# A two-layer hybrid decoder trunk on one core: x also passed transposed, packed weights, and the up-projection's products in another order

## The chip, the core and the metric

The kernel runs on one core of a Trainium2 chip. The metric is the device time of one execution in microseconds (us). A core has a matrix engine (TensorE, PE in the profile, with its weight loads as a row of their own, PEld), a vector engine (DVE), a scalar engine (ACT), GpSimd (POOL) and SyncE (SP), which here issues most of the DMA transfers. All of them run their own instruction lists in order and wait for each other through semaphores.

## What is computed

Two layers over 256 tokens of width 2048. Cut to what the change touches:

```python
def mixer_sublayer(x, ...):
    h = rms_norm(x, attn_norm)
    proj = h @ w_in                       # 12 blocks of columns: q, k, v of three groups of heads,
    (a_q, a_k, a_v, a_f, b_q, b_k, b_v,   # and the latents of the fourth:
     c_q, c_k, c_v, d_cq, d_ckv, d_kr) = jnp.split(proj, offsets, axis=-1)
    ...
    o_d = mla_attention(d_cq, d_ckv, d_kr, ...)   # q = rms_norm(c_q) @ w_uq, kv = rms_norm(c_kv) @ w_ukv
    ...
    return x + y @ w_out

def ffn_sublayer(x, ffn_norm, w_up, conv_w, conv_b, w_down):
    h = rms_norm(x, ffn_norm)
    u = causal_depthwise_conv(h @ w_up, conv_w, conv_b)      # 2048 -> 2 x 5632
    gate, val = jnp.split(u, 2, axis=-1)
    return x + (jax.nn.silu(gate) * val) @ w_down
```

Everything is float32.

## The kernel before

Each float32 factor of a large product is split into a high part and a rest, both in the type fp32r: high = copy of the value in fp32r, low = value minus high. A product of two such factors is then three products on TensorE: high by high, low by high, high by low. Of the weights, ACT makes the high part (line 226) and DVE the low part (line 227), two k-tiles of 128 rows at a time; of the activations, ACT and DVE do the same for hTs (lines 189 and 190), which holds h transposed: for each of 16 k-tiles 128 partitions by [high 256 tokens | low 256 tokens].

**The general product** is the class Gemm (lines 230 to 256). Tokens stand on the output's partitions, two tiles of 128, and up to 512 columns of weights stream through. For each k-tile and each token tile it issues lines 248, 249 and 250.

**The up-projection** is the function up (lines 802 to 825). It has the roles swapped: 128 columns of weights are loaded into the array and the tokens stream through. For each k-tile and each of four column blocks c there is a wide product, the high weights against [high | low] of hTs, 512 columns, and a narrow one, the low weights against high alone, 256 columns, both summed into the bank acc[c]. The two stand in turn, wide, narrow, for c = 0 to 3 (line 812); at the last k-tile the narrow one comes first. There are 22 calls of up in a layer (11 for the gate, tiles up_g, and 11 for the values, up_v), and each issues 16 x 8 = 128 products.

**The start of layer 0** (lines 466 to 485): the block lat (the latents of keys and values, the rotary key and the forget gate, 324 columns) comes first, then dq (the query latent, 512 columns), then aq, uq, ukv, ak and the rest. x is loaded in four chunks of 512 columns in its own layout (line 469), transposed by TensorE (line 201, 32 products), and split by ACT and DVE. For each chunk ACT also sums the squares (line 292) for the norm's factor r_in; that factor is applied when a product leaves its bank. In layer 1 the order of the products is the same, and h comes from the layer before.

**What sets the order.** The code is written as generators (tasks) from which each Gemm and each up takes one or two steps per pair of k-tiles, so that small work (transposes, norms, attention) lies between the large products. A scheduler then orders each engine's instructions. Transfers of weights are issued by SP, one per four k-tiles (line 260), into three buffers raw; the first weights lat0 come in pieces of two k-tiles (lines 222 and 223), each in two transfers, since the four columns of the forget gate lie elsewhere in w_in (lines 461 and 463). A row of a weight tile is a run of 2 KB in memory (512 columns), of 1280 and 16 bytes for lat.

Before the first data are there, TensorE runs 16 products on a tile of zeros, warm (line 105).

Of the kernel before, what the change touches and what calls it, by code (L numbers as in the profile page):

```python
# [24 lines left out]
L = 2  # L25
# [12 lines left out]
OFF_AQ, OFF_AK, OFF_AV, OFF_AF = 0, 512, 1024, 1536  # L38
OFF_BQ, OFF_BK, OFF_BV = 1540, 2052, 2564
OFF_CQ, OFF_CK, OFF_CV = 3076, 3588, 4100  # L40
OFF_DQ, OFF_DKV = 4612, 5124
# [33 lines left out]
def tile_trunk(ctx: ExitStack, tc: tile.TileContext, x, pvec, rows, ctab,  # L75
               w_in, w_uq, w_ukv, w_out, w_up, w_down, out):
# [13 lines left out]
    nc.sync.dma_start(pv[:, 0:KT], pvec[:, 0:KT])  # L90
# [13 lines left out]
    for _ in range(16):  # L104
        nc.tensor.matmul(wps[:, 0:256], warm[:, 0:P], warm, start=True, stop=True)
# [82 lines left out]
    def split_T(ps, j, gain, hi, lo):  # L188
        nc.scalar.activation(hi, ps[:, j * SEQ:(j + 1) * SEQ], AF.Identity, scale=gain)
        nc.vector.scalar_tensor_tensor(lo, ps[:, j * SEQ:(j + 1) * SEQ], gain, hi.bitcast(F32),  # L190
                                       op0=ALU.mult, op1=ALU.subtract)

    def transpose_split(src, n, cnt, gain, kt0, dh, dl):

        for j0 in range(0, cnt, 2):
# [7 lines left out]
            for j in (j0, j0 + 1):  # L203
                split_T(ps, j - j0, gain(j), dh[:, kt0 + j, :], dl[:, kt0 + j, :])
# [6 lines left out]
    def load_weights(src, k, n, nk):  # L211
        loaded[n, k] = wraw.tile([P, 4, 512], F32, tag="raw", name=f"raw_{n}_{k}")
        if n != "lat0":
            src(loaded[n, k], k, min(4, nk))

    def split_weights(src, k, N, n, nk):
# [9 lines left out]
        nc.scalar.copy(hi[:, :, :N], raw[:, :, :N])  # L226
        nc.vector.tensor_tensor(lo[:, :, :N], raw[:, :, :N], hi[:, :, :N].bitcast(F32), op=ALU.subtract)  # L227
        return hi, lo

    class Gemm:  # L230
# [7 lines left out]
        def steps(self, k0, cnt):  # L238
            N = self.N
            for g0 in range(k0, k0 + cnt, 2):  # L240
                hi, lo = split_weights(self.wsrc, g0, N, self.n, self.nk)
                parts = [(*self.act(g0 + i), hi[:, i, :N], lo[:, i, :N]) for i in range(2)]
                for t in range(NT):
                    o = self.acc[t][:, :N]
                    for i, (ah, al, wh, wl_) in enumerate(parts):
                        first, last = self.done + i == 0, self.done + i == self.nk - 1
                        sh, sl = ah[:, t * P:(t + 1) * P], al[:, t * P:(t + 1) * P]
                        nc.tensor.matmul(o, sh, wh, start=first, stop=False)  # L248
                        nc.tensor.matmul(o, sl, wh, start=False, stop=False)  # L249
                        last_mm[0] = nc.tensor.matmul(o, sh, wl_, start=False, stop=last)  # L250
# [43 lines left out]
    def x_ready(c, n, gname, l, ssq, r, rb=None):  # L294
# [3 lines left out]
        yield  # L298
        for t in range(NT):
# [155 lines left out]
    for l in range(L):  # L455
        wl = w_in[l]


        def lat_src(raw, k, cnt):
            rows_ = wl[k * P:(k + cnt) * P]  # L460
            nc.sync.dma_start(raw[:, :, :LATW],
                              rows_[:, OFF_DKV:OFF_DKV + LATW].rearrange("(a p) n -> p a n", p=P))
            nc.sync.dma_start(raw[:, :, LATW:LATF],
                              rows_[:, OFF_AF:OFF_AF + H].rearrange("(a p) n -> p a n", p=P))
        lat_gemm = Gemm(f"lat{l}", LATF, hT, lat_src, KT)
        for c in range(4):
            if l == 0:
# [7 lines left out]
        if l == 0:  # L475
            load_weights(wcols(wl, OFF_DQ, QR), 0, "dq0", KT)
            nc.sync.dma_start(pv[:, KT:], pvec[:, KT:])
            load_rows(0)
# [463 lines left out]
```

## Time and profile before

| | us |
|---|---|
| median of 3 runs | 2268.99 (2268.87 to 2269.32) |
| the profiled execution, its own time | 2267.43 |
| its span (first to last instruction) | 2265.3 |
| TensorE busy in it | 2257.2 |
| ScalarE / VectorE busy | 1197.3 / 1515.4 |

Rows of the timeline give an instruction's start and how long it took from there. On TensorE the products overlap: one that streams 512 columns is listed with 0.39 us while the next starts 0.23 us later. So the pace of TensorE is read from the difference between two starts, not from the listed durations. "x8" in a row means eight products in a row that read alike. The windows view sums busy time over a stretch; its count of products includes those that overlap its edges.

### The profile page before, as it was taken

The page shows a single profiled execution, that of the slowest core. Times are in us where ns is not written, and L with a number is a line of the kernel's source. Part 1 is how long each engine was busy: PE and PEld are TensorE (multiplying, and loading weights), DVE is VectorE, ACT ScalarE, POOL GpSimd, SP SyncE. Part 2 cuts the span into 40 slices and gives each one's busy share as a digit, 9 for nine tenths or more (in the row PEclk, how much of TensorE's full clock was granted, in tenths as well). Part 3 has the DMA queues.
Part 4 walks back from the last instruction along what each step waited for, and adds up shares of the span by engine and source line. Part 5 has one row for each costly group of instructions (what it writes and reads, how often), then busy time and mean ns, then how long its engine had stood idle before and what let it go on. Part 6 is the DMA issues. An engine that isn't in the chain of part 4 may idle for free.

```text
span 2265.3 us, 29605 instructions
## 1 busy us (share of the span) xinstructions
PE 2257.2 (100%) x11632; PEld 1913.5 (84%) x11632; DVE 1515.4 (67%) x2206; ACT 1197.3 (53%) x1738; POOL 1.2 (0%) x7
## 2 busy tenths in 40 slices
PE   9999999999999999999999999999999999999999
PEld 7888888888888888888888888888888888888887
DVE  5766875677656766577657658667776476755674
ACT  6555545555435554455555555455554355534552
POOL 0000000000000000000000000000000000000000
PEclk9999999999999999999999999999999999999999
DMA  7545445555565555555565445455555555555554
GB/s 261 185 143 165 161 159 186 181 191 183 189 195 192 181 192 188 186 190 182 176 191 191 137 161 168 154 183 178 191 187 197 193 185 187 186 191 190 195 168 167
DMA packets 213467, 412.72 MB, mean 182 GB/s; under 512 B 11088, under 2 KB 16464, under 8 KB 213328
## 3 DMA queue, kind: packets, MB, share of 16 engines
q1 hardware_dynamic: 212752, 409.79, 55.0%
q8 instruction: 91, 1.49, 0.3%
q10 hardware_dynamic: 576, 1.05, 0.1%
q14 instruction: 48, 0.39, 0.0%
HBM read 408.71 MB, written 2.10 MB: 181 GB/s over the span
## 4 chain that ended last, share of the span: by engine, by line
PE 99%; DVE 0%; ACT 0%; SPq 0%; DMA 0%; issue 0%; ACTq 0%; DVEq 0%
PE up_v L819 22%; PE up_g L819 22%; PE acc_dn L248 7%; PE acc_dn L250 7%; PE acc_dn L249 7%; PE acc_out L250 2%; PE acc_out L248 2%; PE acc_out L249 2%; PE acc_bk L250 1%; PE acc_cq L250 1%; PE acc_bk L248 1%; PE acc_av L248 1%; PE acc_av L250 1%; PE acc_cq L248 1%; PE acc_bq L248 1%; PE acc_cq L249 1%
## 5 line engine op out<-in xcount | busy, mean ns | idle before, releaser
L819 PE MATMUL up_g<-hTs,hi_g 128*128 128x512 f32 x1408 | 498.4, 398 | 0.0
L819 PE MATMUL up_v<-hTs,hi_v 128*128 128x512 f32 x1408 | 498.1, 398 | 0.0
L819 PE MATMUL up_v<-hTs,lo_v 128*128 128x256 f32 x1408 | 391.7, 281 | 0.0
L819 PE MATMUL up_g<-hTs,lo_g 128*128 128x256 f32 x1408 | 391.2, 280 | 0.0
L227 DVE TENSOR_TENSOR lo_dn<-raw_dn,hi_dn 128x1024 fp32r<-128x1024 f32 x176 | 214.5, 1224 | 190.4 <-ACT hi_dn L226 190.4
L819 PEld LDWEIGHTS up_v<-hTs,hi_v 128*128 128x128 f32 x1408 | 264.5, 188 | 62.9
L819 PEld LDWEIGHTS up_g<-hTs,hi_g 128*128 128x128 f32 x1408 | 264.5, 188 | 62.9
L227 DVE TENSOR_TENSOR lo_v<-raw_v,hi_v 128x1024 fp32r<-128x1024 f32 x176 | 213.4, 1223 | 155.2 <-ACT hi_v L226 155.2
L226 ACT CAST hi_dn<-raw_dn 128x1024 fp32r<-128x1024 f32 x176 | 185.3, 1053 | 243.6 <-PE acc_dn L249 211.2
L227 DVE TENSOR_TENSOR lo_g<-raw_g,hi_g 128x1024 fp32r<-128x1024 f32 x176 | 213.9, 1223 | 136.5 <-ACT hi_g L226 135.3
L226 ACT CAST hi_g<-raw_g 128x1024 fp32r<-128x1024 f32 x176 | 184.8, 1050 | 193.3 <-PE up_v L819 85.0
L226 ACT CAST hi_v<-raw_v 128x1024 fp32r<-128x1024 f32 x176 | 184.6, 1049 | 179.5 <-PE up_g L819 117.1
L819 PEld LDWEIGHTS up_v<-hTs,lo_v 128*128 128x128 f32 x1408 | 265.9, 189 | 2.0
L819 PEld LDWEIGHTS up_g<-hTs,lo_g 128*128 128x128 f32 x1408 | 265.7, 189 | 2.0
L227 DVE TENSOR_TENSOR lo_out<-raw_out,hi_out 128x1024 fp32r<-128x1024 f32 x64 | 78.3, 1224 | 57.0 <-ACT hi_out L226 54.1
L226 ACT CAST hi_out<-raw_out 128x1024 fp32r<-128x1024 f32 x64 | 67.2, 1049 | 63.1 <-PE acc_out L249 46.5
L248 PE MATMUL acc_dn<-hi_dn,a1h_f 128*128 128x512 f32 x192 | 75.0, 390 | 0.0
L248 PE MATMUL acc_dn<-hi_dn,a0h_f 128*128 128x512 f32 x192 | 74.9, 390 | 0.0
L248 PE MATMUL acc_dn<-hi_dn,a2h_f 128*128 128x512 f32 x192 | 74.8, 390 | 0.0
L250 PE MATMUL acc_dn<-lo_dn,a0h_f 128*128 128x512 f32 x192 | 74.8, 390 | 0.0
L249 PE MATMUL acc_dn<-hi_dn,a0l_f 128*128 128x512 f32 x192 | 74.8, 389 | 0.0
L250 PE MATMUL acc_dn<-lo_dn,a1h_f 128*128 128x512 f32 x192 | 74.7, 389 | 0.0
(570 smaller groups left out, 4301.0 us busy)
## 6 DMA issues: line engine op xcount, KB each, us to landing
raw_g<-in_w_up_dram SPq DMA_DIRECT2D x88, 1024.0 KB, 5.0
raw_v<-in_w_up_dram SPq DMA_DIRECT2D x88, 1024.0 KB, 5.0
raw_dn<-in_w_down_dram SPq DMA_DIRECT2D x88, 1024.0 KB, 5.1
raw_out<-in_w_out_dram SPq DMA_DIRECT2D x32, 1024.0 KB, 5.1
raw_dq<-in_w_in_dram SPq DMA_DIRECT2D x8, 1024.0 KB, 5.1
raw_aq<-in_w_in_dram SPq DMA_DIRECT2D x8, 1024.0 KB, 5.0
raw_ak<-in_w_in_dram SPq DMA_DIRECT2D x8, 1024.0 KB, 5.0
raw_av<-in_w_in_dram SPq DMA_DIRECT2D x8, 1024.0 KB, 5.0
```

The source lines that it names most:

```text
L226: nc.scalar.copy(hi[:, :, :N], raw[:, :, :N])
L227: nc.vector.tensor_tensor(lo[:, :, :N], raw[:, :, :N], hi[:, :, :N].bitcast(F32), op=ALU.subtract)
L248: nc.tensor.matmul(o, sh, wh, start=first, stop=False)
L249: nc.tensor.matmul(o, sl, wh, start=False, stop=False)
L250: last_mm[0] = nc.tensor.matmul(o, sh, wl_, start=False, stop=last)
L819: last_mm[0] = nc.tensor.matmul(o, w, a, start=first and whole, stop=last and whole)
```

## The change

Five parts, the first four of which touch only where data stand in memory and the first 50 us or so:

1. x is passed a second time, transposed (xT). In layer 0 hTs is made from xT, without transposes on TensorE; x in its own layout is loaded later, for the sums of squares and the residual.
2. In both layers dq stands ahead of lat. In layer 0 the norm's factor comes during lat; dq's result leaves its banks after that.
3. All weights are packed on the host, so that a transfer of four k-tiles is one run of 8 KB per partition instead of four of 2 KB, and lat's 324 columns lie together.
4. The start: the first pv transfer and the weights of the first k-tile of dq go on ACT's queue; dq's first tiles come in smaller pieces; 24 warm products instead of 16; the rest of pv, the rows, and one part of the tables (tri1, upper) come in the middle of lat, the other part (masks, cosines) after aq's weights.
5. In up, for each k-tile the four wide products stand first and then the four narrow ones.

```diff
-    for _ in range(16):
+    for _ in range(24):
         nc.tensor.matmul(wps[:, 0:256], warm[:, 0:P], warm, start=True, stop=True)
...
-        if n == "lat0":
-            src(raw, k, 2)
+        pieces = [slice(0, 2)]
+        if n == "dq0" and k == 0:
+            pieces = [slice(0, 1), slice(1, 2)]
+            src(raw, 0, 1, nc.scalar)
+            src(raw[:, 1:], 1, 1)
+        elif n == "dq0" and k < 8:
+            src(raw, k, 2)
...
-    def wcols(w, c0, N, row0=0):
-        def src(raw, k, cnt):
-            nc.sync.dma_start(raw[:, :cnt, :N],
-                              w[row0 + k * P:row0 + (k + cnt) * P, c0:c0 + N].rearrange("(a p) n -> p a n", p=P))
+    def wchunk(w, k0=0):
+        def src(raw, k, cnt, q=nc.sync):
+            q.dma_start(raw[:, :cnt, :w.shape[2]], w[:, k0 + k:k0 + k + cnt, :])
         return src
...
+        dq_gemm = Gemm(f"dq{l}", QR, hT, wc["dq"], KT)
+        lat_gemm = Gemm(f"lat{l}", LATF, hT, wchunk(w_lat[l]), KT)
+        if l == 0:
+            for c in range(4):
+                xc = slot(c, "h", [P, 4, SEQ], F32, f"xT_{c}")
+                for j0, j1 in ((0, 2), (2, 4)) if c == 0 else ((0, 4),):
+                    nc.sync.dma_start(xc[:, j0:j1, :], xT[:, 4 * c + j0:4 * c + j1, :])
+                    for j in range(j0, j1):
+                        k = 4 * c + j
+                        split_T(xc[:, j, :], pcol(0, "attn", k), hTs[:, k, 0], hTs[:, k, 1])
+                    dq_gemm.steps(4 * c + j0, j1 - j0)
+            for c in range(4):
+                load_weights(lat_gemm.wsrc, 4 * c, "lat0", KT)
                 for t in range(NT):
                     nc.sync.dma_start(xs[:, t, c * 512:(c + 1) * 512],
                                       x[t * P:(t + 1) * P, c * 512:(c + 1) * 512])
-                for _ in x_ready(c, "in", "attn", 0, ssq_x, rs):
+                for _ in x_stats(c, "in", ssq_x, rs):
                     pass
-            lat_gemm.steps(4 * c, 4)
+                lat_gemm.steps(4 * c, 4)
+                if c == 1:
+                    nc.sync.dma_start(pv[:, KT:], pvec[:, KT:])
+                    load_rows(0)
+                    nc.sync.dma_start(ct[:, CT["tri1"]:], ctab[:, CT["tri1"]:])
...
-                    for c in range(4):
-                        wh, wlo = hi[:, i, c * P:(c + 1) * P], lo[:, i, c * P:(c + 1) * P]
-                        big_mm = (acc[c], wh, hTs[:, k].rearrange("p a s -> p (a s)"))
-                        small_mm = (acc[c][:, :SEQ], wlo, hTs[:, k, 0])
-                        first, last = k == 0, k == KT - 1
-                        for o, w, a in ((small_mm, big_mm) if last else (big_mm, small_mm)):
-                            whole = o.shape[-1] == 512
-                            last_mm[0] = nc.tensor.matmul(o, w, a, start=first and whole, stop=last and whole)
+                    first, last = k == 0, k == KT - 1
+                    cols = [slice(c * P, (c + 1) * P) for c in range(4)]
+                    wide = [(acc[c], hi[:, i, cols[c]], hTs[:, k].rearrange("p a s -> p (a s)")) for c in range(4)]
+                    narrow = [(acc[c][:, :SEQ], lo[:, i, cols[c]], hTs[:, k, 0]) for c in range(4)]
+                    for o, w, a in narrow + wide if last else wide + narrow:
+                        whole = o.shape[-1] == 512
+                        last_mm[0] = nc.tensor.matmul(o, w, a, start=first and whole, stop=last and whole)
```

**Order on TensorE inside up**, where the first gate block of layer 0 takes up its second pair of k-tiles (up_g_0_0 to up_g_0_3 are the four banks, hi_g and lo_g the two parts of the weights). Before:

```order
L819 MATMUL up_g_0_1_3649<-hTs,hi_g_0_2_3683 128x512
L819 MATMUL up_g_0_1_3649<-hTs,lo_g_0_2_3684 128x256
L819 MATMUL up_g_0_2_3650<-hTs,hi_g_0_2_3683 128x512
L819 MATMUL up_g_0_2_3650<-hTs,lo_g_0_2_3684 128x256
L819 MATMUL up_g_0_3_3651<-hTs,hi_g_0_2_3683 128x512
L819 MATMUL up_g_0_3_3651<-hTs,lo_g_0_2_3684 128x256
```

In the changed kernel, at the same place:

```order
L839 MATMUL up_g_0_1_3620<-hTs,hi_g_0_2_3654 128x512
L839 MATMUL up_g_0_2_3621<-hTs,hi_g_0_2_3654 128x512
L839 MATMUL up_g_0_3_3622<-hTs,hi_g_0_2_3654 128x512
L839 MATMUL up_g_0_0_3619<-hTs,lo_g_0_2_3655 128x256
L839 MATMUL up_g_0_1_3620<-hTs,lo_g_0_2_3655 128x256
L839 MATMUL up_g_0_2_3621<-hTs,lo_g_0_2_3655 128x256
L839 MATMUL up_g_0_3_3622<-hTs,lo_g_0_2_3655 128x256
```

Sizes that alternated now come in runs of four; the number of products and their operands are the same.

**Order on TensorE behind the warm products**, at the start of the program. Before (tr_in are the transposes of x, acc_lat the banks of lat):

```order
L105 MATMUL wps<-warm 128x256
L201 MATMUL tr_in_0_119<-ident,xs 128x128 x4
L201 MATMUL tr_in_2_128<-ident,xs 128x128 x4
L248 MATMUL acc_lat_0_115<-hi_lat_0_144,hTs 128x324
L249 MATMUL acc_lat_0_115<-hi_lat_0_144,hTs 128x324
```

In the changed kernel, at the same place:

```order
L105 MATMUL wps<-warm 128x256
L256 MATMUL acc_dq_0_123<-hi_dq_0_136,hTs 128x512
L257 MATMUL acc_dq_0_123<-hi_dq_0_136,hTs 128x512
L256 MATMUL acc_dq_1_124<-hi_dq_0_136,hTs 128x512
L257 MATMUL acc_dq_1_124<-hi_dq_0_136,hTs 128x512
L258 MATMUL acc_dq_0_123<-lo_dq_0_137,hTs 128x512
```

The transposes are gone, and the first large product is one of dq.

**Order on ACT in the changed kernel**, from its first instruction (a0h_xT and a1h_xT are chunks of xT, raw_dq the weights as loaded):

```order
L90 DMA pv<-in_pvec_dram 128x16
L94 ACT_TABLE_LOAD
L269 DMA raw_dq_0_133<-in_w_in_dram 128x512
L189 ACTIVATE hTs<-a0h_xT_127,pv 128x256 x2
L231 CAST hi_dq_0_136<-raw_dq_0_133 128x512
L189 ACTIVATE hTs<-a0h_xT_127,pv 128x256
L231 CAST hi_dq_0_136<-raw_dq_0_133 128x512
L189 ACTIVATE hTs<-a0h_xT_127,pv 128x256
L231 CAST hi_dq_2_160<-raw_dq_0_133 128x1024
```

Two transfers now stand on ACT's list, the second of them behind the load of the activation table, which was ACT's first instruction before.

## Rows read from the trace of the kernel before

**Rows 1.** The page, parts 1 and 4: engines, and the last chain's share by engine.

```profile
PE 2257.2 (100%) x11632; PEld 1913.5 (84%) x11632; DVE 1515.4 (67%) x2206; ACT 1197.3 (53%) x1738; POOL 1.2 (0%) x7
...
PE 99%; DVE 0%; ACT 0%; SPq 0%; DMA 0%; issue 0%; ACTq 0%; DVEq 0%
```

**Rows 2.** Windows, TensorE, 28 up blocks: stretch, length, busy (products), clock, DMA share, GB/s.

```profile
668.62:848.58 179.96, 179.96 (x1025) 1.00 0.56 187
...
sum 631.04, PE 631.04; mean PE 157.76
```

**Rows 3.** Windows, TensorE: two single up blocks, then a down-projection of 384 products.

```profile
668.62:690.82 22.20, 22.20 (x129) 1.00 0.57 190
780.80:803.40 22.60, 22.60 (x130) 1.00 0.56 188
581.56:668.62 87.06, 87.06 (x386) 1.00 0.59 193
```

**Rows 4.** Timeline (start, duration, engine, line, operation), end of an up block, down-projection behind.

```profile
581.33 0.39 PE L819 MATMUL up_v<-hTs,hi_v 128*128 128x512 f32 x1
581.56 0.39 PE L248 MATMUL acc_dn<-hi_dn,a0h_f 128*128 128x512 f32 x1
581.78 0.39 PE L249 MATMUL acc_dn<-hi_dn,a0l_f 128*128 128x512 f32 x1
582.01 0.40 PE L250 MATMUL acc_dn<-lo_dn,a0h_f 128*128 128x512 f32 x1
582.25 0.39 PE L248 MATMUL acc_dn<-hi_dn,a0h_f 128*128 128x512 f32 x1
...
582.94 0.39 PE L248 MATMUL acc_dn<-hi_dn,a0h_f 128*128 128x512 f32 x1
```

**Rows 5.** Timeline, TensorE, first and last of 24 narrow products of uq.

```profile
81.63 0.28 PE L248 MATMUL acc_uq<-hi_uq,a0h_cq 128*128 128x256 f32 x1
...
84.39 0.28 PE L250 MATMUL acc_uq<-lo_uq,a0h_cq 128*128 128x256 f32 x1
```

**Rows 6.** Timeline, TensorE, the start; in brackets the idle time before and its releaser.

```profile
1.09 3.60 PE L105 MATMUL wps<-warm 128*128 128x256 bf16 x16 [1.09 <-DVE warm L102]
4.48 0.42 PE L201 MATMUL tr_in<-ident,xs 128*128 128x128 f32 x1
...
8.62 0.41 PE L248 MATMUL acc_lat<-hi_lat,hTs 128*128 128x324 f32 x1 [1.68 <-ACT hTs L189]
9.51 0.41 PE L249 MATMUL acc_lat<-hi_lat,hTs 128*128 128x324 f32 x1 [0.47 <-DVE hTs L190]
```

**Rows 7.** Windows, all engines (PE, PEld, DVE, ACT, POOL, clock, DMA), inside lat.

```profile
10.50:13.70 3.20, 3.20 (x14) 3.17 (x13) 2.06 (x3) 2.37 (x7) 0.00 (x0) 0.50 1.09 346
```

**Rows 8.** Timeline, TensorE, four successive products of lat, first and last.

```profile
18.41 0.31 PE L248 MATMUL acc_lat<-hi_lat,hTs 128*128 128x324 f32 x1
...
18.85 0.45 PE L248 MATMUL acc_lat<-hi_lat,hTs 128*128 128x324 f32 x2
```

**Rows 9.** Timeline, TensorE: transposes inside dq, and the first product of aq.

```profile
41.96 1.03 PE L523 MATMUL ck<-ident,fb 128*128 128x128 f32 x8
42.75 0.48 PE L249 MATMUL acc_dq<-hi_dq,hTs 128*128 128x512 f32 x1
...
53.50 0.39 PE L248 MATMUL acc_aq<-hi_aq,hTs 128*128 128x512 f32 x1
```

**Rows 10.** DMA view of the first 60 us: issues, KB each, median us to landing.

```profile
raw_lat<-in_w_in_dram SPq DMA_DIRECT2D x8, 320.0 KB, 4.5
xs<-in_x_dram SPq DMA_DIRECT2D x8, 256.0 KB, 4.1
```

**Rows 11.** Timeline, ACT: the table load, and a cast of weights.

```profile
0.73 1.28 ACT L94 ACT_TABLE_LOAD   x1 [0.73 <-PEq L931]
...
24.90 1.04 ACT L226 CAST hi_dq<-raw_dq 128x1024 fp32r<-128x1024 f32 x1
```

**Rows 12.** Windows, all engines, the stretch with the most transfers.

```profile
20.00:28.00 8.00, 7.87 (x51) 7.08 (x50) 5.36 (x10) 6.81 (x14) 0.00 (x0) 1.00 1.03 395
```

More of the change, by code (lines that the diff above doesn't have):

```diff
@@ L74, in tile_trunk @@
 @with_exitstack
-def tile_trunk(ctx: ExitStack, tc: tile.TileContext, x, pvec, rows, ctab,
-               w_in, w_uq, w_ukv, w_out, w_up, w_down, out):
+def tile_trunk(ctx: ExitStack, tc: tile.TileContext, x, xT, pvec, rows, ctab,
+               w_lat, w_in, w_uqn, w_uqr, w_ukv, w_out, w_up, w_down, out):
     nc = tc.nc
@@ L242, in steps @@
                 parts = [(*self.act(g0 + i), hi[:, i, :N], lo[:, i, :N]) for i in range(2)]
-                for t in range(NT):
+                order = [(t, i) for t in range(NT) for i in range(2)]
+                if self.n == "dq0" and g0 == 0:
+                    order = [(t, i) for i in range(2) for t in range(NT)]
+                for t, i in order:
                     o = self.acc[t][:, :N]
[L245 to L250, printed above, removed]
+                    ah, al, wh, wl_ = parts[i]
+                    first, last = self.done + i == 0, self.done + i == self.nk - 1
+                    sh, sl = ah[:, t * P:(t + 1) * P], al[:, t * P:(t + 1) * P]
+                    nc.tensor.matmul(o, sh, wh, start=first, stop=False)
+                    nc.tensor.matmul(o, sl, wh, start=False, stop=False)
+                    last_mm[0] = nc.tensor.matmul(o, sh, wl_, start=False, stop=last)
                 self.done += 2
@@ L298, in x_ready, with x_stats @@
         yield
+        yield from x_stats(c, n, ssq, r, rb)
+    def x_stats(c, n, ssq, r, rb=None):
         for t in range(NT):
@@ L470, in tile_trunk, with cq_task @@
                                       x[t * P:(t + 1) * P, c * 512:(c + 1) * 512])
-                for _ in x_ready(c, "in", "attn", 0, ssq_x, rs):
+                for _ in x_stats(c, "in", ssq_x, rs):
                     pass
-            lat_gemm.steps(4 * c, 4)
-        acc = lat_gemm.acc
[L475 to L478, printed above, removed]
-            nc.sync.dma_start(ct, ctab)
-        finish(h_task[3])
+                lat_gemm.steps(4 * c, 4)
[3 more added lines that the diff above has]
+                    nc.sync.dma_start(ct[:, CT["tri1"]:], ctab[:, CT["tri1"]:])
+        else:
+            for c in range(4):
+                dq_gemm.steps(4 * c, 4)
+            finish(h_task[3])
+        cqT = act_slots(0, f"cq{l}")
+        ss_lat = small("ss_lat", f"{l}", 4)
+        r_lat = small("r_lat", f"{l}", 4)
+        cq = evac(dq_gemm.acc, f"cq{l}", QR, rs, "qk", 2)
+        def cq_task(l=l):
+            for t in range(NT):
+                sumsq(cq[:, t, :], f"cq{l}_{t}", ss_lat[:, 2 + t:3 + t])
+            rsqrt(r_lat[:, 2:4], ss_lat[:, 2:4], f"cq{l}", 1.0 / QR, 2)
+            yield from transpose_split(cq, f"cq{l}", 4, lambda j: pcol(l, "cq", j), 0, *cqT)
+        t_cq = Task(cq_task())
+        if l > 0:
+            lat_gemm.run()
+        acc = lat_gemm.acc
         rsb = small("rsb", f"{l}", NT)
@@ L571, in tile_trunk @@
         for c in range(2):
-            acc = Gemm(f"ukv{l}_{c}", 512, slotted([ckvT], [t_lat]), wcols(w_ukv[l], c * 512, 512), 2).run()
+            acc = Gemm(f"ukv{l}_{c}", 512, slotted([ckvT], [t_lat]), wchunk(w_ukv[l, c]), 2).run()
             for t in range(NT):
@@ L683, in tile_trunk @@
         t_a = Task(a_attn())
-        qb = gemm512("bq", OFF_BQ, rsb, before=t_d)
+        qb = gemm512("bq", "bq", rsb, before=t_d)
         finish(t_ak)
```

103 lines of the change are left out of this document (48 added, 55 removed).

## The prediction

> **What bounds the kernel now.** I read the page first. TensorE has work on it for 2257 of 2265 us, and the chain that ended last is 99% TensorE [rows 1]. So nothing that only makes ACT, DVE or the transfers cheaper can show, unless TensorE waits for it; what counts is how many products there are, at what pace they start, and where TensorE stands still. The listed durations overlap, so next I took the pace from starts. In a down-projection 384 products of 512 columns take 87.06 us, 0.2267 us each [rows 3]. In uq 24 products of 256 columns start from 81.63 to 84.39, 23 steps, 0.120 each [rows 5]. In lat 324 columns take (18.85 - 18.41) / 3 = 0.147 [rows 8]. Then up, which holds nearly half of all time: a block is 64 pairs of a wide and a narrow product, which at these two paces would be 64 x 0.3467 = 22.19 us. One block takes just that, 22.20; another, of the same instructions, 22.60 [rows 3]. The mean over 28 undisturbed blocks is 631.04 / 28 = 22.54 [rows 2]. So alternating sizes cost something in most blocks, 0.34 us in the mean, though the engine never idles. Last I read the start: the first large product stands at 8.62 us, a second waits until 9.51 [rows 6], from 10.5 to 13.7 the granted clock is 0.50, the lower of TensorE's two levels, 1.2 GHz, behind that thin stretch [rows 7], and aq begins at 53.50 [rows 9].
>
> **Part 1: order in up.** No product is added or removed. A group of eight now takes 22.54 / 16 = 1.409 us in the mean; there are 2 x 22 x 16 = 704 groups. The trace has no run of four wide and four narrow, so I bound it by neighbours. *From below:* if every product goes at the pace of its own size, a group is 4 x 0.2267 + 4 x 0.120 = 1.387, the same as in the fast block (22.20 / 16); the gain is 0.022 x 704 = 15 us. *What comes right behind alternation:* where a down-projection follows up, the wide products don't go at 0.2267 at once. From the last wide one of up the starts are 581.33, .56, .78, 582.01, 582.25: four steps in 0.92 us, and seven steps to 582.94 in 1.61, 0.230 each [rows 4]. The pace settles only after some seven wide products. A run of four, behind narrow ones, would never get out of that. The narrow run of uq stood behind wide products and was at 0.120 [rows 5]. So a group is 0.92 + 0.48 = 1.400, and the gain is 0.0086 x 704 = 6 us. *From above:* the dearest wide step of those rows is 582.01 to 582.25, 0.24; four of these give 0.96 + 0.48 = 1.44, a loss of 0.031 x 704 = 22 us. I take 6, because those rows are the nearest: wide products in a row, just behind narrow ones. Both ends stay for the range, the upper one with little weight, since 0.24 stands alone among steps of 0.22 and 0.23. Two small things cost nothing here: a bank's last product now comes 0.3 us later against the block's end, but the next block uses the other four banks; and low weights are needed later than before, not earlier.
>
> The Trainium skill (page "TensorE: Matmul & The Clock Gate", section "Back-to-back issue gap") gives a product's step as its columns over the clock plus 2.5 ns, whatever stands beside it. By that, a pair is an estimated 0.325 us in any order and part 1 is worth nothing. Rows 3 show otherwise, equal instructions in 22.20 and 22.60 us; the measurement decides, and the case in which order doesn't pay stands below as a rival, priced from rows.
>
> **Part 2: the start.** I count to the first product of aq, then add what moves behind it.
> - *First dq product.* The warm products start at 1.09 and the 16 of them end their steps at 4.48, 0.212 each [rows 6]; 24 last until 6.2. Data: xT's first piece is now SP's first transfer, at about 0.8; 4.1 us from issue to landing [rows 10] gives 4.9, and its split is over before the weights come. The weights of k-tile 0 are on ACT's list behind the pv transfer and the table load of 1.28 us [rows 11], so issued at about 2.4; with 4.1 they land at 6.5 in the worst case, with some 3 us, as light traffic may give, at 5.5. A cast of half of 1.04 us [rows 11] follows. I take 6.5 for the first product.
> - *dq and lat.* 96 x 0.2267 = 21.8 and 96 x 0.147 = 14.1, in all 35.9, to 42.4. Some of the first products will run at the lower clock; before, 3.2 us did [rows 7]. Now nothing thins out behind the warm products, so I take half of that stretch, whose loss is again half: 0.8, to 43.2. Another 1.0 for small waits: 44.2.
> - *Behind it.* The transposes and small products of the lat task (4, 8 and 3 of them) lay in dq and now lie in aq; eight transposes take 0.79 us [rows 9], so 1.4 us with the rest. The 32 transposes of x are simply gone; what they took before lies in the 53.50.
>
> 53.50 - 44.2 - 1.4 = 7.9: I take a gain of 8 us. Bounds: a start at 8.6 as now, the old clock stage and 2 us of waits leave 53.5 - (8.6 + 35.9 + 1.6 + 2 + 1.4) = 4; a start at 6.0 with no loss at all gives 53.5 - (6.0 + 35.9 + 1.4) = 10.
>
> **What hides the rest.** The 2.1 MB of xT come on top, but dq needs 4.2 + 2.1 MB in 21.8 us, 289 GB/s; the transfers reached 395 [rows 12]. On ACT four k-tiles of dq need two casts of 1.04 and four splits of under 0.5, some 4 us, against 5.4 us of products. r_in needs all of x and its squares. They run during lat; the last are queued on ACT behind the last cast of lat, and behind them stand dq's leaving its banks and aq's first cast. aq needs dq's banks. By my count dq's banks are free about 2 us before lat ends; without that cover each us of delay costs one. The later first half of the tables stands behind three of aq's four weight transfers on SP; its first use is after ukv, some 20 us on. The packed runs of 8 KB change transfers that take 56% of their engines' time in up [rows 2] and for which TensorE doesn't wait: nothing. In layer 1 dq before lat moves the same work around with TensorE full: nothing, within 0.5 us.
>
> **Sum.** Against the execution in the profile, 2267.4 us (span 2265.3 and 2.1 around it): -6 - 8 = 2253.4. The median of the runs is 1.6 above that execution, so the forecast for the median is 2255.
>
> **Rivals.**
> - *A, order doesn't pay.* Runs of four leave the pace as unsettled as alternation does, 1.409 a group. For it: the wide steps of rows 4 are dear for as long as a run of four lasts. Against: four steps there took 0.92, not 0.93. The start alone remains: 2269 - 8 = 2261.
> - *B, order pays in full.* A group settles at 1.387. For it: one block does so even while it alternates [rows 3], and there are now two changes of size in a group instead of eight. -15 - 8: 2246.
> - *C, slower.* Each wide product behind narrow ones waits for its neighbour, all four at 0.24. Place: every group of up. Price: +22 us, less 8: 2283. It turns the change into a loss once a group passes 1.409 + 8 / 704 = 1.420, a mean wide step of 0.235. For it: single steps of 0.24 in rows 4. Against: they are one in seven.
> - *D, the start doesn't pay.* The transfers of the first 15 us come late: dq falls behind if they bring less than 289 GB/s, and in the early part of lat they moved 346 with 16-byte runs among them [rows 7]. Or dq's banks come free late. The start then gains 0 to 3: 2269 - 6 - 2 = 2261.
> - *E, the scheduler doesn't keep the new order.* The rows printed with the change show the runs of four; the result would be that of A.
>
> The same page of the Trainium skill (section "LDWEIGHTS (loading the stationary operand)") gives 107 ns for loading 128 columns, as long as a narrow product streams at the upper clock; a run of narrow ones would have no slack for its loads, which speaks for C. Rows 5 show 24 narrow products in a row at 0.120, so by the trace the runs bear no such price.
>
> **How the numbers follow.** Forecast 2255 (with its own 4 us on either side) 0.42; B 0.23; A 0.20, with E in it; D 0.09; C 0.04; something else 0.02. The range must leave out no more than 2 in 10: 2246, where B stands, to 2263, just above A and D, leaves out C, the far half of B and the tail of D. Faster or slower by less than 0.2% (4.5 us) is about what can't be told from no change. Forecast, A and B lie below 2264.5, and most of D: faster 0.90. Half of D with A at once: same 0.06. C and the unforeseen: slower 0.04.
>
> **What would show it.** In the changed profile: an up block's length, 22.4 (16 x 1.400) by the forecast, 22.5 by A, 22.2 by B, above 22.7 by C; steps of 0.23 and 0.22 between wide products of one k-tile and 0.12 between narrow ones; the first product of acc_dq near 6.5 us and the first of acc_aq near 44; no long stretch at granted clock 0.50; no idle time of TensorE before acc_aq put down to ACT. I am wrong if blocks take 22.6 or more, if acc_aq begins after 49 us, or if TensorE waits for a DMA inside dq or lat.

## The result and the profile after

The changed kernel takes 2255.17 us (median of 4 runs, 2255.09 to 2255.36); the kernel before, in the same comparison, 2268.93 (2267.47 to 2269.32). The ratio is 0.9941 with a 95% interval of 0.9923 to 0.9958. The forecast was 2255 (2246 to 2263).

The page after, parts 1 and 4, as [rows 1]:

```profile
PE 2246.4 (100%) x11608; PEld 1910.9 (85%) x11608; DVE 1512.6 (67%) x2207; ACT 1180.4 (52%) x1739; POOL 1.2 (0%) x7
...
PE 99%; DVE 0%; DMA 0%; ACT 0%; issue 0%; SPq 0%; DVEq 0%; ACTq 0%
```

TensorE still sets the end. Its span fell from 2265.3 to 2253.4 us. **In up**, windows of TensorE after (stretch, length, busy and products, clock, DMA share, GB/s): seven blocks in a row, then the first block behind a down-projection and the one after it:

```profile
415.95:573.03 157.08, 157.08 (x897) 1.00 0.54 188
...
660.10:682.66 22.56, 22.56 (x130) 1.00 0.55 194
682.66:705.10 22.44, 22.44 (x130) 1.00 0.54 189
```

A block takes 157.08 / 7 = 22.44 us, where [rows 3] had 22.20 or 22.60. All products of up together, from start to start, took 992.6 us before and 988.55 after: 4.05 us less. The timeline of TensorE shows one k-tile of four wide and four narrow products (start, duration, engine, line, operation):

```profile
690.57 0.63 PE L839 MATMUL up_v<-hTs,lo_v 128*128 128x256 f32 x4
691.04 1.09 PE L839 MATMUL up_v<-hTs,hi_v 128*128 128x512 f32 x4
691.97 0.64 PE L839 MATMUL up_v<-hTs,lo_v 128*128 128x256 f32 x4
692.44 1.09 PE L839 MATMUL up_v<-hTs,hi_v 128*128 128x512 f32 x4
```

The group runs from 691.04 to 692.44: 0.93 us for the wide run, 0.47 for the narrow one. At their settled pace four wide products would take 0.907.

**At the start**, TensorE's timeline after (in brackets the idle time before and its releaser), which answers to [rows 6, 9]:

```profile
1.08 4.60 PE L105 MATMUL wps<-warm 128*128 128x256 bf16 x24 [1.08 <-DVE warm L102]
7.40 0.50 PE L256 MATMUL acc_dq<-hi_dq,hTs 128*128 128x512 f32 x1 [1.72 <-ACT hi_dq L231]
...
43.66 0.40 PE L256 MATMUL acc_aq<-hi_aq,hTs 128*128 128x512 f32 x1
...
83.21 0.39 PE L256 MATMUL acc_ak<-hi_ak,hTs 128*128 128x512 f32 x1
```

dq takes from 7.40 to 29.3, lat to 43.66, and ak begins at 83.21 instead of 90.9: 7.7 us are gained by then. From dq's first product on, no stretch of this run is at the lower clock. Most of the warm products are, though: their starts lie 0.213 us apart up to about 4.8 us and 0.110 behind that, while the clock column of the windows reads 1.00 for them too. ACT's timeline shows what the first product waited for:

```profile
1.17 1.28 ACT L94 ACT_TABLE_LOAD   x1 [1.17 <-PEq L964]
1.20 0.42 ACTq L269 DMA_DIRECT2D raw_dq<-in_w_in_dram  x1
4.63 0.91 ACT L189 ACTIVATE hTs<-a0h_xT,pv 128x256 fp32r<-128x256 f32 x2 [2.17 <-DMA pv<-in_pvec_dram]
5.56 0.62 ACT L231 CAST hi_dq<-raw_dq 128x512 fp32r<-128x512 f32 x1
6.33 0.51 ACT L189 ACTIVATE hTs<-a0h_xT,pv 128x256 fp32r<-128x256 f32 x1 [0.16 <-DMA a0h_xT<-in_xT_dram]
6.75 0.60 ACT L231 CAST hi_dq<-raw_dq 128x512 fp32r<-128x512 f32 x1
```

The weights' transfer was issued during the table load, not behind it. The cast of k-tile 0 ended at 6.18; the first product came at 7.40, right behind the cast of k-tile 1, which ended at 7.35.

### The profile page after: what moved, and what is told of

It reads as the page before. It is cut to its first block, busy times and chain, and to the rows that moved or that the text cites. A ratio compares the mean times of both kernels' runs of the same rounds, so it can differ in the third digit from the quotient of the medians.

```text
span 2253.4 us, 29588 instructions
## 1 busy us (share of the span) xinstructions
PE 2246.4 (100%) x11608; PEld 1910.9 (85%) x11608; DVE 1512.6 (67%) x2207; ACT 1180.4 (52%) x1739; POOL 1.2 (0%) x7
## 4 chain that ended last, share of the span: by engine, by line
PE 99%; DVE 0%; DMA 0%; ACT 0%; issue 0%; SPq 0%; DVEq 0%; ACTq 0%
PE up_g L839 22%; PE up_v L839 22%; PE acc_dn L258 7%; PE acc_dn L256 7%; PE acc_dn L257 7%; PE acc_out L258 2%; PE acc_out L256 2%; PE acc_out L257 2%; PE acc_aq L256 1%; PE acc_dq L256 1%; PE acc_bk L258 1%; PE acc_bk L256 1%; PE acc_cq L258 1%; PE acc_av L256 1%; PE acc_cq L256 1%; PE acc_cq L257 1%
## 5 line engine op out<-in xcount | busy, mean ns | idle before, releaser
L839 PE MATMUL up_g<-hTs,hi_g 128*128 128x512 f32 x1408 | 385.9, 395 | 0.0
L839 PE MATMUL up_v<-hTs,hi_v 128*128 128x512 f32 x1408 | 383.9, 394 | 0.0
L839 PEld LDWEIGHTS up_v<-hTs,hi_v 128*128 128x128 f32 x1408 | 242.2, 189 | 33.9
L839 PEld LDWEIGHTS up_g<-hTs,hi_g 128*128 128x128 f32 x1408 | 242.1, 189 | 33.9
L839 PEld LDWEIGHTS up_g<-hTs,lo_g 128*128 128x128 f32 x1408 | 213.8, 189 | 28.3
L839 PEld LDWEIGHTS up_v<-hTs,lo_v 128*128 128x128 f32 x1408 | 213.1, 189 | 28.0
L839 PE MATMUL up_g<-hTs,lo_g 128*128 128x256 f32 x1408 | 221.5, 281 | 0.0
L839 PE MATMUL up_v<-hTs,lo_v 128*128 128x256 f32 x1408 | 220.5, 281 | 0.0
L258 PE MATMUL acc_dn<-lo_dn,a2h_f 128*128 128x512 f32 x192 | 74.7, 389 | 0.0
```

The costliest lines, as they stand in the source:

```text
L839: last_mm[0] = nc.tensor.matmul(o, w, a, start=first and whole, stop=last and whole)
```

## The experiments

**Is the gain the sum of two independent parts?** The first run puts only the new order in up into the kernel before; the second takes only that order back out of the changed kernel.

```diff
-                    for c in range(4):
...
-                        for o, w, a in ((small_mm, big_mm) if last else (big_mm, small_mm)):
+                    for o, w, a in narrow + wide if last else wide + narrow:
```

> The kernel before with the new order in up alone (four wide, four narrow), start untouched. If the changed kernel's gain of 13.8 us is the sum of two independent parts, this one brings what up's blocks show: 22.59 us (most blocks before) to 22.44 (after), times 44 blocks less those that were at 22.20 before: 4 to 5 us, time 2264.5, and the first product of acc_aq stays at 53.5 us. If up's blocks became shorter for another reason (the packed weights, which move the same bytes in longer runs), the blocks stay at 22.5 to 22.6 and the time at 2269.

It took 2263.06 us, ratio 0.9976 (0.9966 to 0.9985). TensorE's windows: two stretches at the start, still at the lower clock as in [rows 7], and the seven blocks; then its timeline at aq:

```profile
10.00:12.00 2.00, 2.00 (x9) 0.50 1.06 367
12.00:14.00 2.00, 2.00 (x9) 0.50 1.12 319
...
424.00:581.08 157.08, 157.08 (x897) 1.00 0.55 188
```

```profile
53.92 0.39 PE L248 MATMUL acc_aq<-hi_aq,hTs 128*128 128x512 f32 x1
```

The blocks are those of the changed kernel to the hundredth, with weights that are not packed. So the order alone shortens up, and packing has no part in it.

> The changed kernel with wide and narrow products in turn again in up; start and packing as changed. Independent parts: 7.7 us of the start remain (first product of acc_ak 83.2 us instead of 90.9), blocks of up 22.5 to 22.6, time 2261. If packing shortens up's blocks: 22.44, time 2256. If the start's gain is given back later: 2265 or more.

It took 2261.10 us, ratio 0.9967 (0.9955 to 0.998). The seven blocks and the first product of aq:

```profile
415.76:573.91 158.15, 158.15 (x898) 1.00 0.52 187
```

```profile
43.57 0.40 PE L256 MATMUL acc_aq<-hi_aq,hTs 128*128 128x512 f32 x1
```

158.15 / 7 = 22.59: alternation is back, the start's gain stays. The two ratios together take away 0.0024 + 0.0033 = 0.0057, the changed kernel 0.0059, the same within their intervals. The parts are independent. In this run no block at all was at 22.20; before, four of the 44 were, two pairs, each right behind a down-projection. Two stretches of six blocks before, without and with such a pair:

```profile
935.65:1071.21 135.56, 135.56 (x770) 1.00 0.56 187
2061.25:2196.03 134.78, 134.78 (x770) 1.00 0.57 188
```

The four fast blocks are worth 4 x 0.39 = 1.6 us. All products of up take 994.26 us in this run, where the profiled run before took 992.6. The fast block of [rows 3] is thus no property of some blocks, and it doesn't come in every run.

**What makes alternation dear?** One explanation is that a narrow product adds into the bank that the wide one has just written. Here each narrow product goes two banks on, and the sizes still alternate, in 14 of the 16 k-tiles:

```diff
+                    turns = [p for c in range(4) for p in (wide[c], narrow[(c + 2) % 4])]
-                    for o, w, a in narrow + wide if last else wide + narrow:
+                    for o, w, a in narrow + wide if last else wide + narrow if first else turns:
```

> The changed kernel, but in up (all k-tiles but the first and the last) wide and narrow products in turn, each narrow one into the bank two further on, so that no bank is written twice in a row. If alternation was dear because the narrow product adds into the bank that the wide one has just written: blocks 22.2 (every product at its own pace, 64 x 0.3467) to 22.44 us, time 2245 to 2255. If it is the change of size alone, whatever the bank: 22.56 to 22.59 us a block as with one bank, time 2260 to 2261.

It took 2261.26 us, ratio 0.9972 (0.996 to 0.9984). Seven blocks:

```profile
416.07:574.13 158.06, 158.06 (x897) 1.00 0.52 188
```

158.06 / 7 = 22.58: the bank is not the cause, the change of size is. A change of operands is not it either: in runs of four, too, each product loads other weights, and a down-projection, whose products are all 512 wide, changes between high and low parts at 0.2267 us [rows 3, 4]. The next two runs ask how its price goes with the length of a run. In the first, every odd k-tile has its narrow products first; in the second, pairs of k-tiles take turns like that.

```diff
-                    for o, w, a in narrow + wide if last else wide + narrow:
+                    for o, w, a in narrow + wide if k % 2 else wide + narrow:
```

> The changed kernel, but in up every odd k-tile has its four narrow products first, so that runs of eight of a size stand in a row. Settling (each run of wide products behind narrow ones pays about 31 ns over its first five products, narrow ones pay nothing): half as many runs, a block of 22.09 + 8 x 0.031 = 22.34 us, 4.4 us less than the changed kernel, 2250.8. Price per change of size (line through 22.59 at 127 changes and 22.44 at 31): 22.42 a block, 1.1 us less, 2254. If the low weights are needed too early (DVE late): TensorE idle in up, slower than the changed kernel.

```diff
+                    todo[0] += [(k, acc[c], hi[:, i, cols[c]], hTs[:, k].rearrange("p a s -> p (a s)")) for c in range(4)]
+                    todo[1] += [(k, acc[c][:, :SEQ], lo[:, i, cols[c]], hTs[:, k, 0]) for c in range(4)]
-                    for o, w, a in narrow + wide if last else wide + narrow:
+                for k, o, w, a in todo[1] + todo[0] if g0 % 4 else todo[0] + todo[1]:
```

> The changed kernel, but in up a pair of k-tiles has its eight wide products first and the next pair its eight narrow ones first: runs of sixteen. Settling: 22.09 + 4 x 0.031 = 22.21 us a block, 10 us less than the changed kernel, 2245. Price per change of size: 22.40, 1.8 us less, 2253.4. If the low weights are needed too early: TensorE idle in up, slower.

They took 2251.29 us, ratio 0.9924 (0.9911 to 0.9936), and 2248.58, ratio 0.9912 (0.9899 to 0.9926). Seven blocks with runs of eight, and the same with runs of sixteen:

```profile
416.02:572.45 156.43, 156.43 (x898) 1.00 0.52 189
```

```profile
417.81:573.68 155.87, 155.87 (x898) 1.00 0.52 190
```

These are 22.35 and 22.27 us a block. The first is what settling was to give (22.34), and far from the price per change of size (22.42). The second lies between the two forecasts, 22.21 and 22.40, and nearer the first. What was off there was the floor: I had put 22.09, with narrow products at the 0.1185 us that they take in runs of four; in long runs they go at 0.120, and the floor is the 22.19 of the prediction. Above that floor a block pays 0.40 us with 63 runs of wide products, 0.25 with 15, 0.16 with 8 and 0.08 with 4: per run 0.006, 0.017, 0.020 and 0.020. A run of eight has paid all there is to pay.

The steps between starts, each a mean over all full runs in up, say the same. In runs of eight, the steps behind the first five wide products are 0.2334, 0.2358, 0.2284, 0.2325 and 0.2308 us, and from the sixth on 0.2267. The first two narrow ones take 0.1134 and 0.1191, the rest 0.120. In the changed kernel's runs of four the wide steps are 0.2347, 0.2345, 0.2319 and 0.2284: such a run ends before it settles.

A block behind that is worth a last run, which also holds ACT's order at the start (below): four k-tiles at a time, runs of 32.

```diff
-            for g0 in range(0, KT, 2):
-                hi, lo = split_weights(src, g0, 512, n, KT)
+            for g0 in range(0, KT, 4):
+                for k2 in (g0, g0 + 2):
+                    hi, lo = split_weights(src, k2, 512, n, KT)
...
+                for k, o, w, a in todo[1] + todo[0] if g0 % 8 else todo[0] + todo[1]:
```

> The kernel with ACT's order held, and in up four k-tiles at a time: sixteen wide and sixteen narrow, the next four k-tiles the other way round, so that runs of 32 stand in a row. The shorter runs gave a net price per run of wide products of 0.020 us (blocks of 22.35 with 8 such runs, 22.27 with 4, both over 64 x 0.3467 = 22.19). Settling: 22.19 + 2 x 0.020 = 22.23 us a block, 9.2 us less in up than the changed kernel; with 0.4 to 1.1 us at the start, 2245 to 2245.6. If the buffers for the weights' two parts (four of each) become the limit, since four k-tiles are held at a time: TensorE idle in up for a DVE or ACT release, blocks longer than 22.27.

It took 2245.85 us (2245.51 to 2245.97), ratio 0.9903 (0.989 to 0.9917), the best of the study and some 9 us under the changed kernel. Seven blocks, and two whole runs in its timeline:

```profile
415.65:571.24 155.59, 155.59 (x898) 1.00 0.53 190
```

```profile
460.10 3.79 PE L859 MATMUL up_v<-hTs,hi_v 128*128 128x512 f32 x16
463.73 4.00 PE L859 MATMUL up_v<-hTs,lo_v 128*128 128x256 f32 x32
467.56 2.68 PE L859 MATMUL up_v<-hTs,hi_v 128*128 128x512 f32 x11
```

22.23 us a block, as settling said, and no sign that the buffers run out. The narrow run is 3.83 / 32 = 0.1197 a product.

The Trainium skill (page "TensorE: Matmul & The Clock Gate", section "Back-to-back issue gap") gives the gap of a single product as its columns over 2.4 GHz plus 2.5 ns, an estimated 215.8 and 109.2 ns here, and for a stream of loads and products of 512 columns about 131 ns; neither has a part for the size of the neighbours. The prediction used the first for a stream. The fp32r products agree with neither: settled steps are 0.2267 and 0.120 us, 11 ns above the formula for both sizes, and the order of equal products moves a block from 22.59 to 22.23 us. Only the last warm products, 256 columns in bf16, go by the formula, 0.109 to 0.110 us apart.

**What at the start brings the 7.7 us?** Four runs each undo one part of the changed start. First, TensorE transposes x again, within dq:

```diff
-                    nc.sync.dma_start(xc[:, j0:j1, :], xT[:, 4 * c + j0:4 * c + j1, :])
+                for _ in transpose_split(xs[:, :, c * 512:(c + 1) * 512], f"in_{c}", 4,
+                                         lambda j: pcol(0, "attn", 4 * c + j), 4 * c, hTs[:, :, 0], hTs[:, :, 1]):
+                    pass
```

> The changed kernel, but x in layer 0 is loaded in its own layout and transposed by TensorE within dq, as before it was within lat; the rest as changed. If the start's gain comes from xT: 32 transposes at 0.1 us are 3.2 us of TensorE back, and the first product of dq comes at 8.6 us or later instead of 7.4, with the low clock behind it or without (0 to 1.6): 4.4 to 6 us more, 2260 to 2261. If it comes from the order dq before lat, the packing and the warm products: 2255 to 2256.

It took 2263.14 us, ratio 0.9978 (0.9969 to 0.9987), 8.0 more than the changed kernel and more than I expected. TensorE's timeline:

```profile
9.02 0.33 PE L200 MATMUL tr_in<-ident,xs 128*128 128x128 f32 x1 [1.99 <-DMA xs<-in_x_dram]
9.80 0.73 PE L256 MATMUL acc_dq<-hi_dq,hTs 128*128 128x512 f32 x2 [0.46 <-ACT hTs L189]
...
51.51 0.40 PE L256 MATMUL acc_aq<-hi_aq,hTs 128*128 128x512 f32 x1
```

The first product is 2.4 us later, the transposes stand inside dq again, and the lower clock is back (0.50 from 12 to 14 us); dq takes 27.4 us instead of 21.9. How these 5.4 us divide among transposes, waits and clock, the run doesn't tell. The run is as long as the one with the order in up alone (2263.06). So dq first, packing, the pieces and eight more warm products bring nothing together unless x comes transposed. Now lat ahead of dq, with xT:

```diff
-                    dq_gemm.steps(4 * c + j0, j1 - j0)
+                    lat_gemm.steps(4 * c + j0, j1 - j0)
...
-                lat_gemm.steps(4 * c, 4)
+                dq_gemm.steps(4 * c, 4)
```

> The changed kernel, but with lat ahead of dq in layer 0 again, xT kept, the small first pieces moved to lat. Lat needs 2.65 MB of weights and 2.1 MB of xT in 14.1 us, 337 GB/s, where dq first needs 289 GB/s; the transfers reached 395. If the order of the two doesn't matter beside xT: first product of acc_aq at 43.7 us, time 2255.2. If lat first outruns the transfers: TensorE waits in lat for raw_lat or xT, 1 to 3 us more, 2256 to 2258. If the norm's factor, now ready earlier, was what mattered: up to 0.5 us less.

It took 2255.56 us, ratio 0.9946 (0.9933 to 0.996). The transfers do show, but cost little. ACT's timeline, then TensorE's:

```profile
8.90 1.71 ACT L189 ACTIVATE hTs<-a1h_xT,pv 128x256 fp32r<-128x256 f32 x4 [1.15 <-DMA a1h_xT<-in_xT_dram]
```

```profile
11.28 0.41 PE L256 MATMUL acc_lat<-hi_lat,hTs 128*128 128x324 f32 x1 [0.67 <-ACT hi_lat L231]
...
44.22 0.39 PE L256 MATMUL acc_aq<-hi_aq,hTs 128*128 128x512 f32 x1
```

aq begins 0.56 us later than in the changed kernel. The longest wait on the way, 0.67 us, is for a cast that stands on ACT's list behind a piece of xT, for which ACT itself waited 1.15 us. The median differs by 0.4 us, which this comparison can't tell from nothing. Next, the warm products:

```diff
-    for _ in range(24):
+    for _ in range(16):
```

> The changed kernel with 16 warm products instead of 24. They end at about 4.5 us and TensorE stands until the first product of dq at 7.4. In one profiled run of this study, with 2.05 us of idle time there instead of 1.72, the granted clock then fell to about 0.5 from 8.4 to 11.8 us and dq took 23.5 us instead of 21.9. If the length of that pause decides: the low clock comes in every run, 1.0 to 1.7 us more than the changed kernel, 2256.5. If the eight warm products do nothing: 2255.2, clock 1.00 throughout.

It took 2257.47 us, ratio 0.9954 (0.9941 to 0.9966). TensorE's timeline:

```profile
1.08 3.60 PE L105 MATMUL wps<-warm 128*128 128x256 bf16 x16 [1.08 <-DVE warm L102]
7.38 0.80 PE L256 MATMUL acc_dq<-hi_dq,hTs 128*128 128x512 f32 x1 [2.70 <-ACT hi_dq L231]
7.97 0.63 PE L257 MATMUL acc_dq<-hi_dq,hTs 128*128 128x512 f32 x1
8.40 0.63 PE L256 MATMUL acc_dq<-hi_dq,hTs 128*128 128x512 f32 x1
```

Steps of 0.43 us instead of 0.23, up to 12.2 us: dq takes 24.3 us instead of 21.9, and the whole 2.3 more. The loss is larger than I wrote, because the engine is at the lower of its two levels from its first warm product on: all sixteen start 0.213 us apart. In the changed kernel the upper level came at about 4.8 us, within the eight further warm products; here they are missing, and it came only behind dq's first products. How much of that is due to the eight products, and how much to the longer pause, the run doesn't separate. Last, the weights in rows again, four runs of 2 KB where the changed kernel moves one of 8 KB:

```diff
-        return w.reshape(L, -1, P, w.shape[2] // n, n).transpose(0, 3, 2, 1, 4)
+        return w.reshape(L, -1, P, w.shape[2])
...
+            ap = ap.rearrange("l a p (c n) -> l c p a n", n=wide_rows[n])
```

> The changed kernel with the weights in rows again, as before: a transfer of four k-tiles is four runs of 2 KB per partition instead of one of 8 KB (lat's columns stay together). If packing is hidden, as I forecast: 2255.2, first product of acc_aq at 43.7 us, blocks of up 22.44. If the start, where the transfers are busy for the whole of dq and lat, needs the longer runs: TensorE waits in dq or lat, acc_aq at 44.5 to 46, 1 to 2 us more, 2256 to 2257; up unchanged.

It took 2255.57 us (2255.10 to 2256.77), ratio 0.9947 (0.9933 to 0.996). Three of the five runs lie between 2255.1 and 2255.6, as the changed kernel; two lie at 2256.6 and 2256.8, of which one is the profiled run. Its windows (all engines; the clock is third from the end) show why, and so do those of the profiled run with runs of sixteen, which took 2249.76 where two others of its four runs took 2247.75 and 2247.76:

```profile
8.00:12.00 4.00, 4.00 (x13) 3.15 (x12) 3.61 (x8) 3.65 (x7) 0.00 (x0) 0.61 1.03 397
```

```profile
8.00:12.00 4.00, 4.00 (x11) 3.16 (x12) 3.74 (x8) 3.85 (x8) 0.00 (x0) 0.57 1.01 393
```

Both had 2.05 us of idle time between the warm products and dq's first; the profiled runs that had 0.85 to 1.76 there kept clock 1.00. So packing itself is hidden, as forecast. The start of the changed kernel, though, leaves a pause that varies from run to run, and two of the profiled runs with this start fell to the lower level behind it, at a price of 1 to 2 us.

**What holds the first product of dq?** Two runs. In the first the two k-tiles of the first pair have tiles of their own; in the second ACT's list is also held in the order of need.

```diff
-        hi = wspl.tile([P, 2, 512], F32R, tag="hi", name=f"hi_{n}_{k}")
         for s in pieces:
+            hi = wspl.tile([P, 2, 512], F32R, tag="hi", name=f"hi_{n}_{k}_{s.start}")
```

> The changed kernel, but the two k-tiles of the first pair of dq have weight tiles of their own, instead of two halves of one. In the changed kernel the cast of the first half ended at 6.18 us, that of the second at 7.35, and the first product came at 7.40. If it waited for the second half only because the two share a tile: first product at about 6.3, and 0.3 to 1.1 us less in all (VectorE's low parts may be the next limit), 2254.1 to 2254.9. If something else held it (the weight load, xT): first product at 7.4, 2255.2.

It took 2255.20 us, ratio 0.9945 (0.9933 to 0.9958); four of the five runs lie between 2254.87 and 2255.23, one at 2257.87. ACT's timeline, then TensorE's:

```profile
4.30 0.91 ACT L189 ACTIVATE hTs<-a0h_xT,pv 128x256 fp32r<-128x256 f32 x2 [1.84 <-DMA pv<-in_pvec_dram]
6.14 0.51 ACT L189 ACTIVATE hTs<-a0h_xT,pv 128x256 fp32r<-128x256 f32 x1 [0.93 <-DMA a0h_xT<-in_xT_dram]
6.55 1.12 ACT L232 CAST hi_dq<-raw_dq 128x512 fp32r<-128x512 f32 x2
```

```profile
7.21 0.50 PE L263 MATMUL acc_dq<-hi_dq,hTs 128*128 128x512 f32 x1 [1.54 <-ACT hi_dq L232]
```

The product now starts before the second cast has ended (6.55 + 1.12 = 7.67), so the shared tile did hold it. But the scheduler put a third part of xT ahead of both casts, ACT waited 0.93 us for that, and the gain was gone.

```diff
+    pin = tc.keep_in_program_order
...
-            nc.scalar.copy(hi[:, s, :N], raw[:, s, :N])
+            keep(nc.scalar.copy(hi[:, s, :N], raw[:, s, :N]))
```

> As the run with own tiles for the first two k-tiles of dq, but with ACT's list for the first four k-tiles held in the order in which TensorE needs it: part of xT, cast of k-tile 0, part of xT, cast of k-tile 1, and so on (with own tiles alone, ACT had a third part of xT ahead of the first cast and waited 0.93 us for it). If the two together held the first product: it comes at 6.2 to 6.4 instead of 7.4, VectorE or ACT become the limit behind it, and the whole is 0.4 to 1.1 us shorter, 2254.1 to 2254.8, without a run at the low clock, since the pause behind the warm products shrinks to under 1 us. If not: first product at 7.2 to 7.4, 2255.2.

It took 2254.74 us (2254.66 to 2255.17), ratio 0.9943 (0.9931 to 0.9956). TensorE's timeline here, and in the run with runs of 32, which has the same start:

```profile
6.57 0.50 PE L269 MATMUL acc_dq<-hi_dq,hTs 128*128 128x512 f32 x1 [1.12 <-ACT hi_dq L238]
```

```profile
6.16 0.50 PE L269 MATMUL acc_dq<-hi_dq,hTs 128*128 128x512 f32 x1 [0.71 <-ACT hi_dq L238]
...
9.53 0.50 PE L269 MATMUL acc_dq<-hi_dq,hTs 128*128 128x512 f32 x1 [0.35 <-ACT hi_dq L238]
```

The first product comes 0.8 to 1.2 us earlier, but lat begins at 28.9 and 29.2 us instead of 29.3. The second pair of k-tiles is late next: in the second of these runs ACT waited 0.36 us for its transfer. Most of what an earlier start gains is lost to later waits, and the 0.4 us between the medians of this run and the changed kernel can't be told from nothing. What is left is that the pause shrinks to about 1 us, and all nine runs with this start lie close together (2254.66 to 2255.17, 2245.51 to 2245.97). The four of the changed kernel do so too, so that the shorter pause is what keeps them together is not shown.

## Why the prediction was right, and where it was not

**The time and its reason.** 2255 was forecast, 2255.17 measured, with the two parts named and both of about the size given: between the profiles, 4.05 and 7.7 us for 6 and 8. Rivals A to E fell: blocks at 22.44 are neither 22.54 nor 22.20, the start paid, and the order in up was kept.

**Two misses cancel, in part by luck.** From profile to profile I forecast 14 us, and 12.2 came (2267.43 to 2255.23, the profiled run's own time after). Then I added 1.6 us, because the median before lay that far above its profiled run; after, the median is that of the profiled run. Without that, the forecast would have been 1.8 us too low. The record suggests one root for both: the four fast blocks of the profiled run before are worth 1.6 us, as much as it lies below the median. That the other runs before had fewer of them is not shown, since only the profiled one has a trace. From median to median 13.8 us came.

**Part 1, the term that was mis-sized.** The step was "So a group is 0.92 + 0.48 = 1.400". It is 0.9295 + 0.474 = 1.4035 (sums of the mean steps above), against 1.409 a gain of 0.0055 x 704 = 3.9 us. The mechanism was right: a run of four doesn't settle. But I had read the wide steps from a single place [rows 4], where the timeline's hundredths left 0.92 or 0.93 open (0.93 is what I had given to rival A), and had taken the narrow run of uq, whose 23 steps are mostly settled [rows 5]; the first narrow products behind wide ones are shorter. The 1.409 was off too: the 28 blocks of [rows 2] hold all four fast ones. Without fast blocks a group in turn takes 22.59 / 16 = 1.412, and against the run that only has the new start, which had none, the order gains 994.26 - 988.55 = 5.7 us, close to my 6; the medians of the two runs lie 5.9 us apart. The size came out right by errors on both sides of the difference.

**The rest of part 1.** "Two small things cost nothing" missed a third. In the first block behind a down-projection the four banks come from that projection. The fourth wide product now needs its bank 0.7 us after the block's start instead of 1.05 (before, the first and the fourth start at 668.62 and 669.67). In the changed kernel's timeline TensorE is held there until VectorE's last add out of these banks ends (659.56 + 1.41 = 660.97):

```profile
660.08 0.84 PE L839 MATMUL up_g<-hTs,hi_g 128*128 128x512 f32 x3
660.76 0.40 PE L839 MATMUL up_g<-hTs,lo_g 128*128 128x256 f32 x2
661.02 0.50 PE L839 MATMUL up_g<-hTs,hi_g 128*128 128x512 f32 x1
```

```profile
659.56 1.41 DVE L808 TENSOR_TENSOR xs<-xs,acc_dn 128x512 f32<-128x512 f32 x2
```

That is 22.56 - 22.44 = 0.12 us in each of four blocks, 0.5 us.

**Part 2, step by step.** The first product came at 7.40, not 6.5. Two things that I had worked out were wrong: the weights' transfer doesn't queue behind the table load, and the first product waits for both casts. A third I had not looked at: ACT's first work waits 2.17 us for pv, which took 3.9 us from issue to landing where it had taken 1.8 on SP's queue before. And the warm products ended at 5.7 us, not at 6.2, because their last steps were at the upper level; so the pause behind them was 1.72 us where my numbers left 0.3. The losses behind it were 0.4 us instead of 1.8, since the lower clock didn't come in that run and small waits were few: 7.40 + 35.9 + 0.4 = 43.7 against 44.2. Of the lat task, 24.86 - 22.69 = 2.2 us moved into aq, not 1.4. The three errors, +0.9, -1.4 and +0.8, leave 7.7 instead of 7.9. The bounds of 4 to 10 held, but the clock, which I treated as half a loss, came in the profiled runs with this start either not at all or for some eight products of dq.

**What was to be hidden was hidden.** Packing: the run in rows. dq's banks: in ACT's timeline they are emptied from 40.05 to 41.3 us, 2.3 before lat's end, where "about 2" stood. TensorE has no idle time before aq. Layer 1: dq, lat and aq take 22.71 + 15.01 + 23.89 us after, lat, dq and aq 15.01 + 23.89 + 22.69 before: 0.02 apart.

**What stays open.** Why a wide product behind a narrow one starts the next one up to 9 ns later, and why that lasts for five products, no run tells; nor why alternation now and then runs at the settled pace for the two blocks behind a down-projection [rows 3], at two of four such places in one profile and at none in another.

## What to carry over

When TensorE never idles, read its pace from start to start and compare equal blocks with each other: a block that takes 22.20 and 22.60 us with the same instructions shows a price of order. If products of two sizes feed the same sums, put them in runs, and turn every second group round, so that the ends of two groups meet in one size: that doubles a run and costs no buffer. At a start, ask for each early step what comes late next; a first product that starts 1 us earlier gained less than these runs can tell from nothing, and what counted there was work that disappeared altogether (the transposes), and that TensorE reached the upper level in its warm products and kept it through the pause behind them.

## What the runs showed of the hardware

- A run of wide products behind narrow ones pays about 27 ns over its first five products, and the narrow run behind it gets back some 8 ns on its first two: 0.02 us net for each run of eight or more, 0.006 where every run is one product long. Products into the same bank one behind the other cost no more than into different ones (22.59 and 22.58 us a block).
- The warm products begin at the lower level, 0.213 us from start to start. With 24 of them the changed kernel's profile reaches the upper one, 0.110 us, at about 4.8 us; with 16 they ended before, and dq's first eleven products went at the lower level as well, with steps of 0.43 us, up to 12.2 us. In the run with the order alone 16 were enough: its last two warm steps are 0.110 and 0.109.
- Behind 24 warm products, TensorE stood for 0.85, 1.39, 1.54, 1.72 and 1.76 us in five profiled runs whose dq stayed at the upper level (and for 0.71, 0.90 and 1.12 in three with another start), and for 2.05 us in two that then ran some eight of dq's first products at the lower level. The clock column of the windows reads 1.00 for the warm products and for the whole start of the run with 16, so there the steps, and not that column, show the level.
- A transfer issued on ACT's queue went out at 1.20 us, 0.03 us after the start of a table load of 1.28 us that stands ahead of it in ACT's list.
